# A new attention and convolution list, conditioning products in bursts of eight, a gate broadcast by rounded halves, and shorter one-column sums

## The chip, the core and the metric

The kernel runs on one core of a Trainium2 chip. A core has a matrix engine (TensorE, PE in the profile, with its weight loads as PEld), a vector engine (VectorE, DVE), an activation engine (ScalarE, ACT), a general engine (GpSimd, POOL) and a queue engine that issues most transfers (SyncE, SP). Each works through its own list of instructions in order and waits at semaphores for the others. The metric is the time of one execution on the device in microseconds; lower is better.

## What is computed

One layer of a hybrid backbone on 512 latent and 128 context tokens, all in float32 (D = 1024):

```python
mod = (silu(cond) @ w_ada + b_ada)            # cond: c for latents, c_ctx for context
sh1, sc1, g1, sh2, sc2, g2 = split(mod, 6)
h = rms(x, norm_mix) * (1 + sc1) + sh1
q, k, v, gb, gc, u = split(h @ w_in)          # 8 q heads, 2 kv heads of 64; 3 x 512 for the convolution
q, k = rms(q), rms(k)                         # per head; rotary on latents
attn = softmax(q k^T / 8) v                   # latents read cached context keys and all latents, context reads itself
y_conv = gb * conv3(gc * u)
x = x + g1 * (concat(rms(attn), rms(y_conv)) @ w_out)
h2 = rms(x, norm_ffn) * (1 + sc2) + sh2
x = x + g2 * ((silu(h2 @ w_gate) * (h2 @ w_up)) @ w_down)
```

Outputs are the new x of both token sets and the context's k and v.

## The kernel before

Tokens stand in five tiles of 128 (`t` 0 to 3 latents, 4 = `CTX`). Float32 products are done in three passes: each operand is split into a rounded part (`fp32r`, `hi`) and the rest (`lo`), and `mm3` issues hi·hi, hi·lo and lo·hi. `split` puts the rounding on ScalarE and the subtraction on VectorE. A product of two plain float32 operands is built as two records instead.

Four stages follow each other. First (0 to about 56 us) the conditioning for the first norm, the transposition of x, and q. Then the attention and convolution stage (to about 259 us), which the change is in. Then the output projection in two halves of 512 columns, `j` = 0 and 1. Last the feed-forward part, from about 323 us to the end.

In the second stage the order of TensorE is written by hand, as a list `SEQ` of tokens. `k`, `K`: keys and values of a tile, and the transposition of its keys. `q`, `Q`: norm and rotary of a tile's queries on the other engines, and their transposition. `a`, `t`, `o`: context attention's scores, transposition, products. `Su.h`, `Tu.g`, `Ou.g`: scores of head h, transposition and value product of key group g of latent unit u (16 units: tile, kv head, pair of heads). `r`: the one-column sums of a tile's output norm. `F1`: one filler step. The fillers (84 steps) come from a generator: 12 convolution blocks (`conv_mm`, L675 to L677) of six steps, and after each of them one step of `ada_all`, which computes the conditioning of the sections 2, 3 and 4 (the first gate, the second shift and scale; two halves of 512 columns each).

`ada_all`: a section half takes eight products of 32 rows and 512 columns (`cond_mm`, L377), which go to four column strips of the array in turn. They stand as four in one filler step and four in the next. The result `res` is copied by ScalarE. For the gate it is spread over all partitions by a product with `selT` (L737), once for latents and once for context; for the others four small products with `sel` follow (L742). This second part stands at the head of the next step, ahead of the next section's first four products.

`att_rms` (L900) sums the squares `osq` of a tile's attention output over its four blocks of 128 with four products against a column of ones. `conv_rms` does it for the convolution and gives `rB`, which the first mixing step of the projection needs.

The orders of the other engines come from a scheduler that goes by priorities: `early(n)` raises the priority of what is issued under it. `SOON` stands at the softmax steps and at the splits of transposed probabilities, `SOW` at the splits of weights (negative: later). Weight tiles come in rings: `WFB` = 3 loaded ones, `WHB` = 4 split ones, and `AWB` loaded tiles of conditioning weights; each holds two of a section's eight blocks. PSUM in this stage: two buffers of tag `t` for transpositions and sums, three of `c`, one of `o`, one double one of `s` for scores.

Of the kernel before, what the change touches and what calls it, by code (L numbers as in the profile page):

```python
# [10 lines left out]
F32R = mybir.dt.float32r  # L11
AF = mybir.ActivationFunctionType
ALU = mybir.AluOpType
AX = mybir.AxisListType

P = 128
# [18 lines left out]
P1PRE = ('r0 r1 r2 x0 r3 x1 v0 x2 a0 w0 x3 m0 r4 h00 a1 q02 q01 x4 q00 m1 h01 h10 a2 q03 h11 p0 q04 c0')  # L35
XB = 3
XTE = [0, 1, 0, 1, 1, 1, 0, 1, 1, 0]
SEQ = ('k1 c0 q4 k4 C0 k0 K4 Q4 q0 a0 F1 k2 a1 K0 t0 k3 t1 o0 K1 F1 Q0 o1 K2 F1 K3 F1 S0.0 F1 F1 S0.1 '
# [10 lines left out]
GCUT = [0, 6, 12, 17, 22]  # L49
GB = 6  # L50
SOP = [20, 0]
# [9 lines left out]
RSP = 0  # L61
# [8 lines left out]
PHB = 2  # L70
XP = 50
XPL = 400
TAT = (0, 1)
AWB = 2
AO = 6
SOON = 150
SOW = -300
NA = [0, 1]
QTB = 3
WFB = 3  # L80
# [8 lines left out]
def build(ctx, tc, x_prompt, x_sample, c, cache_k, cache_v, c_ctx, norm_mix, norm_ffn, w_ada, b_ada,  # L89
# [3 lines left out]
    act, dve, pool, pe, sp = nc.scalar, nc.vector, nc.gpsimd, nc.tensor, nc.sync  # L93
# [4 lines left out]
    def open_pool(name, side, names):  # L98
        g = tc.tile_pool(name=name, bufs=1, side=side, reuse_waits="tile")
        pools[name] = (g, g.__enter__())  # L100
        for n in names.split():
            where[n] = name
# [14 lines left out]
    def T(tag, shape, dt=F32, bufs=1):  # L117
        seq[0] += 1
        return pools[where.get(tag, "A")][1].tile(list(shape), dt, tag=tag, bufs=bufs, name=f"{tag}_{seq[0]}")
# [21 lines left out]
    def f32(ap):  # L141
        return ap.bitcast(F32)

    def early(n):
        return tc.high_priority(n)

    def split(hi, lo, src):
        act.activation(hi, src, AF.Copy)  # L148
        dve.tensor_tensor(lo, src, f32(hi), ALU.subtract)  # L149
# [65 lines left out]
    def load(e, later=False):  # L215
# [4 lines left out]
        a, b = src.shape[1], src.shape[2]  # L220
        wf = T("aw", (P, a, b), F32, AWB) if ring == "a" else T("wf", (P, a, b), F32, WFB)
        sp.dma_start(wf, src)
# [73 lines left out]
    for gi, grp in enumerate(GROUPS):  # L296
        for f in grp:
            ph = 2 if f < NPLAIN else 3
# [59 lines left out]
    ones = T("ones", (P, P))  # L358
# [11 lines left out]
    dve.tensor_copy(cp[:, :, 0:2], cs)  # L370
    sel = T("sel", (P, CG))
    dve.tensor_reduce(sel, ident.rearrange("p (g c) -> p c g", c=CG), AX.X, ALU.add)
    selT = T("selT", (P, 2, P))

    def cond_mm(out, k, w):
        g = k % 4
# [17 lines left out]
    def mod_evict(i, f0, n, ps_sc, ps_sh):  # L394

        no = (V_MIX, V_FFN)[i]
        bo = (0, 24)[i]
        if ps_sc is not None:
            tmp = T("modt", (P, n, 2), F32, 2)
            dve.tensor_tensor(tmp, ps_sc, vec[:, no + f0:no + f0 + n].unsqueeze(2).to_broadcast([P, n, 2]), ALU.mult)  # L400
            dve.tensor_tensor(modA[i][:, f0:f0 + n, :], tmp,
                              nb[:, i, f0:f0 + n].unsqueeze(2).to_broadcast([P, n, 2]), ALU.add)
        if ps_sh is not None:
            dve.tensor_tensor(modB[i][:, f0:f0 + n, :], ps_sh,
                              vec[:, bo + f0:bo + f0 + n].unsqueeze(2).to_broadcast([P, n, 2]), ALU.add)
# [142 lines left out]
        else:  # L548
            act.activation(qraw[t], qacc[t], AF.Copy)
    close_pool("B0")  # L550
    open_pool("B2", "left", "vt KA KB VS qT pr ph pl osq c25 aw es")
    phase[0] = 1
    close_pool("psum")
    open_psum("pp2", {"t": PT, "c": 5 - PT, "o": 1, "s": 1})
# [7 lines left out]
    for nm, g in (("q", q_norm), ("k", k_norm)):  # L562
# [5 lines left out]
        r4 = rs_.rearrange("p t (a b c) -> p t a b c", a=2, b=2)  # L568
# [36 lines left out]
    KA = T("KA", (P, NKV, 768), F32R)  # L605
    KB = T("KB", (P, NKV, 768), F32R)
    VS = T("VS", (P, 6, NKV, 2, HD), F32R)
# [109 lines left out]
        yield from ada_some(1)  # L717

    def ada_all():
        for sec, j in ADA:  # L720
            rp = PB(tag="c")
            for h in range(4):
                w = W(("ada", sec, j, h))
                for i in range(2):
                    cond_mm(rp, 2 * h + i, w[:, i])
                if h == 1:
                    yield
            res = T("rs5", (P, 512))
            with early(RSP) if RSP else ExitStack():
                act.activation(res, rp, AF.Copy)  # L730
            if sec == 2:
                sp.dma_start(res[2:3], b_ada[0:1, sec * D + j * 512:sec * D + (j + 1) * 512])
            yield
            if sec == 2:
                for cc in range(2):
                    ps = PB(tag="c")
                    pe.matmul(ps, selT[:, cc], res, start=True, stop=True)  # L737
                    act.activation(g1[cc][:, j * 512:(j + 1) * 512], ps, AF.Copy)
            else:
                ps = PB((P, 4, 2), tag="c")  # L740
                for f in range(4):
                    pe.matmul(ps[:, f], res[:, f * P:(f + 1) * P], sel[:, 0:2], start=True, stop=True)  # L742
                if sec == 4:
                    mod_evict(1, 4 * j, 4, ps, None)
                else:
                    mod_evict(1, 4 * j, 4, None, ps)

    ada_gen = ada_all()

# [28 lines left out]
    qT = [None] * NT  # L778
    oe, osq = {}, {}
    mix_ctx = [T("m0", (P, 4, P), F32R, 2) for _ in range(2)]  # L780

    def att_s(u, h):
# [7 lines left out]
        nm = T("nm", (P, 1), F32, 4)  # L790
        with early(SOON):
            dve.tensor_reduce(nm, s_in, AX.XY, ALU.max, negate=True)
        pr = T("pr", (P, NKEY), F32, PRB)
        sm = T("sm", (P, 1), F32, 4)
        with early(SOON):
            act.activation(pr.rearrange("p (a b) -> p a b", a=2), s_in, AF.Exp, bias=nm, accum_out=sm)
        rsm = T("rsm", (P, 1), F32, 4)
        with early(SOON):
            dve.reciprocal(rsm, sm)
# [8 lines left out]
    def att_t(u, g):  # L808
# [7 lines left out]
        pl = T("pl", (P, 2, 2, P), F32R, PHB)[:, :n]  # L816
        with early(SOON):
            split(ph, pl, tp)
# [24 lines left out]
    def att_add(t, v, e):  # L843

        esw = T("es", (P, 2, P))
        sp.dma_start(esw[0:64], e[64:128, :, 0, :])
        sp.dma_start(esw[64:128], e[0:64, :, 1, :])
        if v == 0:
            of[t] = T("of", (P, 4, P), F32, NT)
            osq[t] = T("osq", (P, 4, P), F32, OSQ) if t != NL - 1 else T("oz", (P, 4, P))  # L850
        o = of[t][:, 2 * v:2 * v + 2]
        dve.tensor_tensor(o[0:64], e[0:64, :, 0, :], esw[0:64], ALU.add)
        dve.tensor_tensor(o[64:128], e[64:128, :, 1, :], esw[64:128], ALU.add)
        act.activation(osq[t][:, 2 * v:2 * v + 2], o, AF.Square)
        if t == CTX:
            split(mix_ctx[0][:, 2 * v:2 * v + 2], mix_ctx[1][:, 2 * v:2 * v + 2], o)

# [20 lines left out]
    def ctx_t(v):  # L878
# [4 lines left out]
        pl = T("pl", (P, GRP, P), F32R, PHB)  # L883
        with early(SOON):
            split(ph, pl, tp)
# [10 lines left out]

    def att_rms(t):
        sps = PB((P, 1))
        for p in range(4):
            pe.matmul(sps, osq[t][:, p], ones[:, 0:1], start=(p == 0), stop=(p == 3))  # L900
        rA[t] = rstd_of(sps, 1, 1.0 / 512, tag="rA")

    def unit(t, v, p):
# [10 lines left out]
    def rms_of(t):  # L914
        if t == CTX or t >= 0:
# [5 lines left out]
             "a": ctx_s, "t": ctx_t, "o": ctx_o, "r": att_rms}  # L921
    for x in SEQ.split():
        if "." in x:
# [30 lines left out]
    def h2_turn(t):  # L954
        cc = 1 if t == CTX else 0
        for g in range(2):
# [4 lines left out]
            for i in range(4):  # L961
                k = 4 * g + i
                with early(XPL):
                    act.activation(h2[g][:, i, FPOS[t]:FPOS[t] + P], tp[:, i], AF.Identity,
# [64 lines left out]
    for j in range(2):  # L1029
        cols = slice(j * 512, (j + 1) * 512)  # L1030
        for n, t in enumerate(TORD[j]):
            cc = 1 if t == CTX else 0
            c0 = t * P + (2 if t == CTX else 0)
            ms = [mix_ctx if t == CTX else mix_half(of[t]), mix_half(yf[:, :, c0:c0 + P])]
            ab = PS2()
            for half in range(2):
                for p in range(4):
                    wh, wl = W(("o", j, 2 * half + p // 2))
                    mm3(ab[:, half], ms[half][0][:, p], ms[half][1][:, p], wh[:, p % 2], wl[:, p % 2],
                        p == 0, p == 3)  # L1040
                    if j == 1 and n >= 2 and (half, p) == TAT:
                        h2_turn(TORD[1][n - 2])
                        if n == 3:
                            b_lo(0, 256)
                        if n == 4:
                            with early(XPL):
                                b_lo(256, HALF)
# [9 lines left out]
            if j == 0:  # L1057
                x2[t] = T("x2", (P, D), F32, NT)
                sp.dma_start(x2[t], x_dram[t])
            with early(XP if j == 0 else XPL):  # L1060
                m = T("mix", (P, 512), F32, 2)
# [5 lines left out]
            if j == 1:  # L1067
                with early(XPL):
                    x2n[t] = T("x2n", (P, D), F32, 2)
# [218 lines left out]
```

## Time and profile before

| | |
|---|---|
| median of 3 runs | 760.46 us (760.42 to 761.08) |
| the profiled execution | 759.46 us |
| its span in the profile | 757.7 us |
| instructions in the profile | 13163 |

The times of rows are those of the profiled execution, from the start of its span. Rows of a timeline give start, length, engine, line, operation, and in brackets the idle time just before with what ended it. The end of a matmul is modelled, so that lengths of matmuls overlap and prices are better read from start to start. A chain of waits gives start, length and what was on it. A table of stretches gives busy time with the number of instructions.

### The profile page before, as it was taken

To read this page: it belongs to the slowest core of one execution; us is meant where nothing else is said; L and a number is where in the kernel's file an instruction comes from. 1 tells how busy PE (TensorE), PEld (TensorE's weight loads), DVE (VectorE), ACT (ScalarE), POOL (GpSimd) and SP (SyncE) were. 2 spreads that over 40 slices of the span, in tenths; PEclk is the share of its full clock that TensorE was granted. 3 is DMA by queue.
4 is the path that set the end of the run, shared out by engine and by line. 5 is a ranking of instruction groups with operands and counts; after the bars stand their busy time and mean duration, and the time that the engine had idled before them with its cause. 6 is when DMAs were issued, how large, how long until landed. Compare 5 with 4: busy or idle time off the path is not lost.

```text
span 757.7 us, 13163 instructions
## 1 busy us (share of the span) xinstructions
PE 734.8 (97%) x5225; PEld 688.8 (91%) x5225; DVE 556.9 (73%) x993; ACT 377.0 (50%) x716; POOL 49.6 (7%) x77
## 2 busy tenths in 40 slices
PE   4998999999999999999999999999999999999997
PEld 3677888989998887889999999999999999999997
DVE  5566987676665799779879778874577866788663
ACT  5455767566656435896552225653125542255510
POOL 2104201011000150000000000000000000000000
PEclk9999999999999999999999999999999999999999
DMA  9994133522433464031235313133213232222312
GB/s 288 310 248 133 43 112 92 171 93 91 142 124 91 133 222 139 1 112 56 84 89 176 112 56 111 57 112 112 57 56 90 79 112 68 73 84 85 112 56 84
DMA packets 102354, 84.60 MB, mean 112 GB/s; under 512 B 4526, under 2 KB 82674, under 8 KB 102292
## 3 DMA queue, kind: packets, MB, share of 16 engines
q1 hardware_dynamic: 100980, 83.39, 36.4%
q8 instruction: 41, 0.67, 0.4%
q10 hardware_dynamic: 1056, 0.26, 0.2%
q0 software_dynamic: 256, 0.11, 0.1%
q14 instruction: 21, 0.17, 0.1%
HBM read 79.68 MB, written 2.75 MB: 109 GB/s over the span
## 4 chain that ended last, share of the span: by engine, by line
PE 83%; DVE 7%; DMA 4%; SPq 2%; ACT 1%; issue 1%; POOL 1%; ACTq 0%; DVEq 0%; POOLq 0%
PE pf L1189 19%; PE pf L153 12%; PE pf L154 12%; PE pf L152 12%; PE pc L675 3%; PE pc L677 3%; PE pc L676 3%; PE po L831 3%; PE ps L788 2%; PE ps L152 2%; PE pt L814 2%; PE ps L154 2%; PE ps L153 2%; PE pc L377 2%; DMA af<-in_w_ada_dram 2%
## 5 line engine op out<-in xcount | busy, mean ns | idle before, releaser
L1189 PE MATMUL pf<-wh,gT 128*128 128x256 f32 x880 | 137.1, 277 | 0.0
L1189 PEld LDWEIGHTS pf<-wh,gT 128*128 128x128 f32 x880 | 117.1, 188 | 0.5 <-issue 0.2
L148 ACT ACTIVATE wh<-wf 128x1024 fp32r<-128x1024 f32 (+1 forms) x76 | 64.3, 846 | 90.0 <-PE pf L1189 45.1
L1189 PE MATMUL pf<-wl,gT 128*128 128x256 f32 x440 | 86.5, 276 | 0.0
L149 DVE TENSOR_TENSOR wl<-wf,wh 128x1024 fp32r<-128x1024 f32 (+1 forms) x42 | 49.2, 1172 | 27.6 <-ACT wh L148 23.4
L1189 PEld LDWEIGHTS pf<-wl,gT 128*128 128x128 f32 x440 | 66.6, 188 | 0.0
L675 PE MATMUL pc<-hH,wh 128*128 128x384 f32 (+1 forms) x192 | 61.5, 320 | 0.2 <-DVE modt L400 0.2
L676 PE MATMUL pc<-hL,wh 128*128 128x384 f32 (+1 forms) x192 | 59.5, 310 | 0.0
L677 PE MATMUL pc<-hH,wl 128*128 128x384 f32 (+1 forms) x192 | 59.4, 309 | 0.0
L152 PE MATMUL pf<-T,wl 128*128 128x320 f32 x160 | 49.2, 308 | 0.0
L153 PE MATMUL pf<-T,wl 128*128 128x320 f32 x160 | 49.2, 308 | 0.0
L154 PE MATMUL pf<-T,wl 128*128 128x320 f32 x160 | 49.2, 308 | 0.0
L152 PE MATMUL pf<-T,wh 128*128 128x320 f32 x160 | 49.2, 308 | 0.0
L153 PE MATMUL pf<-T,wh 128*128 128x320 f32 x160 | 49.2, 308 | 0.0
L154 PE MATMUL pf<-T,wh 128*128 128x320 f32 x160 | 49.2, 308 | 0.0
L152 PE MATMUL pf<-B,wl 128*128 128x320 f32 x152 | 47.0, 309 | 0.0
L153 PE MATMUL pf<-B,wl 128*128 128x320 f32 x152 | 46.8, 308 | 0.0
L154 PE MATMUL pf<-B,wl 128*128 128x320 f32 x152 | 46.8, 308 | 0.0
L148 ACT ACTIVATE wl<-wf 128x512 fp32r<-128x512 f32 x34 | 21.6, 635 | 43.4 <-PE pf L1189 35.5
L152 PE MATMUL pf<-B,wh 128*128 128x320 f32 x136 | 41.9, 308 | 0.0
L153 PE MATMUL pf<-B,wh 128*128 128x320 f32 x136 | 41.9, 308 | 0.0
L154 PE MATMUL pf<-B,wh 128*128 128x320 f32 x136 | 41.9, 308 | 0.0
(278 smaller groups left out, 1958.6 us busy)
## 6 DMA issues: line engine op xcount, KB each, us to landing
wf<-in_w_gate_up_dram SPq DMA_DIRECT2D x44, 512.0 KB, 3.9
aw<-in_w_ada_dram SPq DMA_DIRECT2D x24, 512.0 KB, 4.8
wf<-in_w_down_dram SPq DMA_DIRECT2D x20, 512.0 KB, 3.6
wf<-in_w_in_dram SPq DMA_DIRECT2D x18, 512.0 KB, 6.0
af<-in_w_ada_dram SPq DMA_DIRECT2D x32, 256.0 KB, 6.0
x<-in_x_sample_dram SPq DMA_DIRECT2D x8, 512.0 KB, 4.9
wf<-in_w_out_dram SPq DMA_DIRECT2D x8, 512.0 KB, 4.3
wf<-in_w_ada_dram SPq DMA_DIRECT2D x8, 512.0 KB, 3.7
```

The source lines that it names most:

```text
L148: act.activation(hi, src, AF.Copy)
L149: dve.tensor_tensor(lo, src, f32(hi), ALU.subtract)
L152: pe.matmul(out, lh, rh, start=start, stop=False, skip_group_check=more)
L153: pe.matmul(out, lh, rl, start=False, stop=False, skip_group_check=more)
L154: pe.matmul(out, ll, rh, start=False, stop=stop, skip_group_check=more)
L377: pe.matmul(out[CG * g:CG * (g + 1)], cp[:, k], w, start=(k < 4), stop=(k >= KD - 4), skip_group_check=True)
L675: pe.matmul(acc, wh[:, k], hH[k][:, c0:c0 + n], start=(k == 0), stop=False)
L676: pe.matmul(acc, wh[:, k], hL[k][:, c0:c0 + n], start=False, stop=False)
L677: pe.matmul(acc, wl[:, k], hH[k][:, c0:c0 + n], start=False, stop=(k == KD - 1))
L788: pe.matmul(s2[:, g, :320], q, kk[:, v, P + g * 320:P + (g + 1) * 320], start=(i == 0), stop=(i == 1))
L831: pe.matmul(ov, w, x[:, i].rearrange("p a q -> p (a q)"), start=(g == 0 and i == 0 and n == 0), stop=(last and i == len(kts) - 1 and n == 1))
L1189: pe.matmul(ps[:, c:c + 256], l, r[:, i, c0 + c:c0 + c + 256], start=f == grp[0] and a == 0 and c == 0, stop=f == grp[-1] and a == 2, skip ...
```

## The change

Besides the list `SEQ`, which is written anew from `a0` on, four things. `ada_all` yields once at its head, then does all eight products in one step and the second part in the next one; `AWB` goes from 2 to 4. The gate's `res` is split into `rh` and `rl`, `selT` is rounded (it holds zeros and ones), and each spread is two products of rounded operands. After the second kv head of a tile GpSimd adds the two halves of `osq`, so that `att_rms` needs two products. The priorities of softmax steps and of weight splits move apart.

```diff
-SEQ = ('k1 c0 q4 k4 C0 k0 K4 Q4 q0 a0 F1 k2 a1 K0 t0 k3 t1 o0 K1 F1 Q0 o1 K2 F1 K3 F1 S0.0 F1 F1 S0.1 '
-       'q1 F1 F1 S1.0 F1 T0.0 S1.1 T0.1 T0.2 O0.0 F1 O0.1 O0.2 S2.0 T1.0 F1 T1.1 T1.2 S2.1 O1.0 F1 F1 '
...
+SEQ = ('k1 c0 q4 k4 C0 k0 K4 Q4 q0 a0 k2 F1 a1 t0 K0 k3 K1 o0 t1 F1 Q0 K2 o1 K3 F1 S0.0 F1 F1 S0.1 F1 q1 '
+       'F1 F1 S1.0 F1 T0.0 S1.1 T0.1 F1 T0.2 O0.0 O0.1 S2.0 O0.2 T1.0 F1 T1.1 O1.0 S2.1 T1.2 F1 Q1 F1 '
...
+GSE = 0
-AWB = 2
+AWB = 4
-SOON = 150
-SOW = -300
+SOON = 640
+SOW = -850
...
-    selT = T("selT", (P, 2, P))
+    selT = T("selT", (P, 2, P), F32R)
...
     def ada_all():
+        yield
         for sec, j in ADA:
             rp = PB(tag="c")
             for h in range(4):
                 w = W(("ada", sec, j, h))
                 for i in range(2):
                     cond_mm(rp, 2 * h + i, w[:, i])
-                if h == 1:
-                    yield
             res = T("rs5", (P, 512))
-            with early(RSP) if RSP else ExitStack():
-                act.activation(res, rp, AF.Copy)
+            act.activation(res, rp, AF.Copy)
...
             if sec == 2:
+                hi, lo = T("rh", (P, 512), F32R), T("rl", (P, 512), F32R)
+                with early(GSE):
+                    split(hi, lo, res)
                 for cc in range(2):
                     ps = PB(tag="c")
-                    pe.matmul(ps, selT[:, cc], res, start=True, stop=True)
+                    pe.matmul(ps, selT[:, cc], hi, start=True, stop=False)
+                    pe.matmul(ps, selT[:, cc], lo, start=False, stop=True)
                     act.activation(g1[cc][:, j * 512:(j + 1) * 512], ps, AF.Copy)
...
+            yield
...
         act.activation(osq[t][:, 2 * v:2 * v + 2], o, AF.Square)
+        if v:
+            pool.tensor_tensor(osq[t][:, 0:2], osq[t][:, 0:2], osq[t][:, 2:4], ALU.add)
...
-        for p in range(4):
-            pe.matmul(sps, osq[t][:, p], ones[:, 0:1], start=(p == 0), stop=(p == 3))
+        for p in range(2):
+            pe.matmul(sps, osq[t][:, p], ones[:, 0:1], start=(p == 0), stop=(p == 1))
```

TensorE at the first gate spread, before: `rs` is the section's result, `aw` conditioning weights of the next section, `pt` transposed probabilities `pr`.

```order
L814 MATMUL pt_1636<-ident_76,pr_1544 128x128
L737 MATMUL pc_1647<-rs_351_1467,selT_142 128x512
L737 MATMUL pc_1650<-rs_351_1467,selT_142 128x512
L377 MATMUL pc_1653<-aw_1459,cp_84 32x512 x2
L377 MATMUL pc_1653<-aw_1463,cp_84 32x512 x2
L814 MATMUL pt_1662<-ident_76,pr_1437 128x128
```

And TensorE after the change, first at the first burst of a section with the context tile's sums behind it:

```order
L792 MATMUL ps_1439<-KB_695,qT_1119 128x320 x2
L378 MATMUL pc_1455<-aw_704,cp_84 32x512 x2
L378 MATMUL pc_1455<-aw_718,cp_84 32x512 x2
L378 MATMUL pc_1455<-aw_1243,cp_84 32x512 x2
L378 MATMUL pc_1455<-aw_1245,cp_84 32x512 x2
L906 MATMUL pt_1471<-ones_130,osq_1095 128x1 x2
```

Then at the first gate spread:

```order
L818 MATMUL pt_1635<-ident_76,pr_1550 128x128
L739 MATMUL pc_1650<-rh_1646,selT_142 128x512
L740 MATMUL pc_1650<-rl_1647,selT_142 128x512
L739 MATMUL pc_1654<-rh_1646,selT_142 128x512
L740 MATMUL pc_1654<-rl_1647,selT_142 128x512
L818 MATMUL pt_1658<-ident_76,pr_1446 128x128
```

The burst that stood right behind the gate spread now stands a filler block later, as one of eight products; the sums are two instead of four.

VectorE at the first latent unit, before: `of` is the context attention's output, `KB` the keys' low part from a transposition, `wl` a split of convolution weights, `nm` the maximum of the first scores.

```order
L853 TENSOR_TENSOR of_1096<-t_260_1091,es_1093 64x256
L622 CAST KB_695<-pt_1145 128x2x128
L164 TENSOR_SCALAR rs_1224<-rs_1224 128x8
L598 TENSOR_TENSOR pl_1229<-of_665,tab_682 128x16x16
L149 TENSOR_TENSOR wl_1473<-wf_1470,wh_1472 128x1024
L149 TENSOR_TENSOR m_171_702<-of_1096,m_170_701 128x256
L622 CAST KB_695<-pt_1159 128x2x128
L852 TENSOR_TENSOR of_1096<-t_269_1135,es_1137 64x256
L853 TENSOR_TENSOR of_1096<-t_269_1135,es_1137 64x256
L792 TENSOR_REDUCE nm_1181<-ps_1176 128x1
```

VectorE at the same place after the change:

```order
L857 TENSOR_TENSOR of_1094<-t_258_1089,es_1091 64x256
L623 CAST KB_695<-pt_1132 128x2x128
L623 CAST KB_695<-pt_1153 128x2x128
L165 TENSOR_SCALAR rs_1225<-rs_1225 128x8
L150 TENSOR_TENSOR m_171_702<-of_1094,m_170_701 128x256
L599 TENSOR_TENSOR pl_1230<-of_665,tab_682 128x16x16
L796 TENSOR_REDUCE nm_1172<-ps_1167 128x1
L150 TENSOR_TENSOR wl_1485<-wf_1482,wh_1484 128x1024
```

The two KB follow each other, and the weight split stands behind the maximum.

GpSimd at the end of the stage after the change (`oz` is the last tile's squares, `rB` the convolution's norm):

```order
L717 TENSOR_TENSOR ysum_700<-ysum_700,c_776_3243 128x512
L717 TENSOR_TENSOR ysum_700<-ysum_700,c_776_3243 128x128
L860 TENSOR_TENSOR oz_3033<-oz_3033 128x256
L163 TENSOR_TENSOR rB_3347<-ms_3345,neghalf_132 128x5
L1071 TENSOR_TENSOR mix_3383<-mix_3383,g_167_698 128x512
```

Before, `rB` stood right behind the two `ysum` rows; the add of `oz` is new ahead of it.

More of the change, by code (lines that the diff above doesn't have):

```diff
@@ L550, in build @@
     close_pool("B0")
-    open_pool("B2", "left", "vt KA KB VS qT pr ph pl osq c25 aw es")
+    open_pool("B2", "left", "vt KA KB VS qT pr ph pl osq c25 aw es rh rl")
     phase[0] = 1
```

18 rows, old and new, of the table SEQ are left out of this document.

## Prediction

> **What bounds the kernel now.** I read the page's first part and its chain, then the busy times by stage, then who keeps TensorE waiting, then rows of the timeline for the prices.
>
> ```profile
> span 757.7 us, 13163 instructions
> PE 734.8 (97%) x5225; PEld 688.8 (91%) x5225; DVE 556.9 (73%) x993; ACT 377.0 (50%) x716; POOL 49.6 (7%) x77
> PE 83%; DVE 7%; DMA 4%; SPq 2%; ACT 1%; issue 1%; POOL 1%; ACTq 0%; DVEq 0%; POOLq 0%
> ```
>
> TensorE (PE) holds 83% of the chain that ended last: most time taken from its stream is time taken from the kernel. The stretches of 56 to 75, 75 to 106, 106 to 268 and 268 to 300 us say where this holds (busy us and instruction counts of PE, PEld, DVE, ACT, POOL; then granted clock, DMA share, GB/s):
>
> ```profile
> 56.00:75.00 19.00, 16.90 (x117) 14.97 (x116) 12.31 (x38) 10.53 (x27) 8.76 (x14) 1.00 0.45 135
> 75.00:106.00 31.00, 28.24 (x203) 25.21 (x203) 28.31 (x70) 22.19 (x59) 5.22 (x8) 1.00 0.32 94
> 106.00:268.00 162.00, 161.29 (x1153) 145.45 (x1152) 111.24 (x222) 98.82 (x201) 15.15 (x25) 1.00 0.37 114
> 268.00:300.00 32.00, 31.78 (x137) 24.67 (x136) 30.76 (x43) 14.18 (x23) 8.88 (x6) 1.00 0.58 194
> ```
>
> The attention and convolution list runs from 56 to some 259 us. From 106 us on TensorE is full and VectorE (DVE) has a third of its time free. In 75 to 106 VectorE is the fuller one (28.31 of 31), and there TensorE waits. From 268 to 300, in the output projection, both are full. After that the diff touches nothing. What TensorE itself waited for in the stage (us in total, times, longest), and one wait of ScalarE (ACT):
>
> ```profile
> PE ps L788 <- DVE KB L622: 1.2, 1, 1.2
> PE pt L814 <- DVE pl L149: 0.7, 1, 0.7
> PE pt L655 <- ACT qT L656: 0.7, 1, 0.7
> PE po L831 <- DVE pl L149: 0.4, 1, 0.4
> PE ps L788 <- ACT pr L796: 0.4, 1, 0.4
> ...
> ACT wh L148 <- PE pc L676: 3.1, 3, 1.5
> ```
>
> So two things can move the time: the work in TensorE's stream, and these few waits.
>
> **Bursts of eight.** Before, each of six conditioning sections runs its eight products (L377, four at a time in the four column strips of the array) in two bursts of four, in two filler steps. Now all eight stand in one step, the first ada step of the list is empty and the last burst stands in the last step. The work is the same, so only the edges can be saved:
>
> ```profile
> 25.21 1.07 PE L377 MATMUL pc<-af,cp 128*32 128x256 f32 x16
> 26.21 0.50 PE L152 MATMUL ps<-wh,hH 128*128 128x512 f32 x1
> ...
> 97.48 0.45 PE L788 MATMUL ps<-KB,qT 128*128 128x320 f32 x2
> 97.86 1.06 PE L377 MATMUL pc<-aw,cp 128*32 128x512 f32 x8
> 98.86 0.44 PE L675 MATMUL pc<-hH,wh 128*128 128x384 f32 x1
> 99.14 0.34 PE L676 MATMUL pc<-hL,wh 128*128 128x384 f32 x1
> 99.32 0.34 PE L677 MATMUL pc<-hH,wl 128*128 128x384 f32 x1
> ...
> 100.86 0.45 PE L788 MATMUL ps<-KB,qT 128*128 128x320 f32 x2
> 101.15 0.34 PE L675 MATMUL pc<-hH,wh 128*128 128x384 f32 x1
> ```
>
> Ends of matmuls are modelled, so I go from start to start. Two score products took 0.38 us ahead of a burst (97.48 to 97.86) and 0.29 elsewhere (100.86 to 101.15): 0.09 to get in. The first convolution product behind it took 0.28 (98.86 to 99.14), the next 0.18: 0.10 to get out. Within, a burst of four took 1.00; eight products of half the width took 1.00 as well (25.21 to 26.21), so there the fixed part is nothing; the gate's records below stream 512 columns in 0.43, which makes two rounds 0.86 and the fixed part 0.14. I take 0.10, nearer to the larger since its width is the same. A section saves 0.29, six save 1.7 (ends 0.19 and 0.33: 1.1 to 2.0). The Trainium skill, page "TensorE: Matmul & The Clock Gate", section "Part 3: Packing small matmuls — row/col tiling", has a pack cost one matmul's duration plus some 4 ns for each further tile. By that rule two packs cost the same together or apart and this term would be 0, with the time at 756.2; the rows show the 0.19 at the edges, so they decide. The loads of a section (four of 512 KB) now need four buffers, which they get. They pass convolution weights on the in-order queue of SP, but ScalarE's splits of those wait for TensorE to free their buffers (3.1 us above): they are early, and a load that is some us later costs nothing.
>
> **Gate broadcast by halves.** Two sections each end in two full-precision products against selT, two records each. Now each is two products of rounded halves, one record each, as the 512-column products of the projection are; these start 0.24 apart (second fence, from the chain of waits):
>
> ```profile
> 118.25 0.95 PE L900 MATMUL pt<-ones,osq 128*128 128x1 f32 x8
> 119.05 0.63 PE L814 MATMUL pt<-ident,pr 128*128 128x128 f32 x4
> ...
> 128.51 1.88 PE L737 MATMUL pc<-rs,selT 128*128 128x512 f32 x4
> 130.33 1.06 PE L377 MATMUL pc<-aw,cp 128*32 128x512 f32 x8
> ```
>
> ```profile
> 318.86 0.23 PE ps L152
> 319.10 0.24 PE ps L153
> ```
>
> 1.82 us (128.51 to 130.33) less 0.09 for the entry of the burst behind is 1.73; four records at 0.24 make 0.95; saved 0.78, twice 1.6 (1.4 to 1.7). The split adds one ScalarE and one VectorE instruction of 512 columns per section. A whole filler block lies between burst and gate, and VectorE has 50 us free in 106 to 268, which covers it.
>
> **Fewer one-column sums.** Each of five normalizers took eight records in 0.80 us (118.25 to 119.05); four records take 0.40. Five times is 2.0; the last one stands in the stretch where VectorE is full as well and may be worth nothing (1.6 to 2.2, by 0.11 a record). The price is an add on GpSimd (POOL) per normalizer, below.
>
> **The new order of the list.** Up to a0 (about 75 us) it is the same, and the waits there stay. Then, at the first latent unit (DVE and PE rows, the latter with the idle time in brackets):
>
> ```profile
> 91.74 0.42 DVE L622 CAST KB<-pt 128x256 fp32r<-128x256 f32 x1
> 92.25 0.42 DVE L598 TENSOR_TENSOR pl<-of,tab 128x256 f32<-128x256 f32 x1
> 92.59 1.22 DVE L149 TENSOR_TENSOR wl<-wf,wh 128x1024 fp32r<-128x1024 f32 x1
> 94.06 0.42 DVE L622 CAST KB<-pt 128x256 fp32r<-128x256 f32 x1
> 94.53 0.41 PE L788 MATMUL ps<-KB,qT 128*128 128x320 f32 x1 [1.19 <-DVE KB L622]
> 105.13 0.44 PE L814 MATMUL pt<-ident,pr 128*128 128x128 f32 x2 [0.70 <-DVE pl L149]
> 74.16 0.53 PE L655 MATMUL pt<-identr,qT 128*128 128x128 f32 x4 [0.69 <-ACT qT L656]
> ```
>
> The last KB stood behind a rotary product and a weight split on VectorE. With weight splits at lower priority the two KB now follow each other and the split stands behind nm: the KB comes some 1.9 us sooner and the 1.19 goes. T0.2 needed the buffer of T0.0 after 1.0 us of other work and waited 0.70; a filler step of six 384-column products (0.18 each, 99.14 to 99.32 above) now stands between: it goes. Against that, K2 now follows Q0 at once, with one transposition group between it and the buffer's former use, as at 74.16: up to 0.7 comes. Net -1.2. Covers of the later units (score to score, transposition to product) have a shortest of 2.0 and 1.5 us by the same counting, before 1.8 and 1.2, so I expect no worse there; but 84 fillers have moved and I keep 0.5 for a wait I can't see: -0.7. Ends: -2.7 (the four waits of DVE and of pr all go), +2.7 (as many new ones).
>
> **The sum.** -1.7 - 1.6 - 2.0 - 0.7 = -6.0 on the profiled execution's 759.46, which has 1.76 outside its span: 753.5. The median of the runs stands 1.0 above that execution: 760.46 - 6.0 = 754.5.
>
> **Rivals.**
> (a) The work goes and the new order's waits give part of it back: 5.3 of work less 1.5 to 3.8 of waits, 756.7 to 759.0. For it: the list is new from 75 us on and TensorE has no slack. Against it: VectorE is 69% and ScalarE 61% busy in 106 to 268, and the covers got longer.
> (b) The adds on GpSimd hold up VectorE.
>
> ```profile
> L566 POOL TENSOR_TENSOR tab<-pr,gnq 128x256 f32<-128x256 f32 x1 | 0.7, 728 | 37.1 <-DMA pr<-rope_c_dram 37.1
> L149 DVE TENSOR_TENSOR mL<-of,mH 128x512 fp32r<-128x512 f32 x8 | 7.7, 956 | 0.7 <-ACT mH L148 0.7
> L149 DVE TENSOR_TENSOR mL<-y,mH 128x512 fp32r<-128x512 f32 x10 | 6.8, 682 | 0.2 <-ACT mH L148 0.2
> ```
>
> The same split takes 956 ns on average where GpSimd's gate products run beside some of them, and 682 elsewhere. An add of this size took 0.73, so five hold VectorE at most 3.6 us, and only two fall where it is nearly full: the context tile's and the last tile's, which in addition stands ahead of rB in GpSimd's queue, and rB lets the projection's first mix go. That costs 0.7 to 1.5: 755.2 to 756.0. The Trainium skill, page "SBUF — State Buffer", section "SBUF: two separate sides", says that GpSimd and a VectorE operation with two SBUF inputs exclude each other for a whole instruction; the two rows agree with it.
> (c) Slower: the softmax chains become the bound. Each of the sixteen latent units goes score, maximum, exponential, scaling, transposition, split, product over three engines with two transposition buffers and one score buffer. If the denser stream exposes 0.5 us in each, 8 us come: 762.5. It decides from 0.47 us a unit, since 7.5 have to come back and more. Against it: those units show 0.4 us of named waits after 106 us.
> (d) The saved work isn't on the path, since the projection behind it is held by VectorE (30.76 of 32) with its own backlog. VectorE sat idle waiting for TensorE until the last units, so it moves with it; if not, 759 to 762.
>
> **How the numbers follow.** Sum as worked out (752 to 756.5, with (b) inside): 0.64. (a) 0.20. (d) and a full give-back, within 0.2% (1.5 us, about what a measurement of this kernel can tell from no change): 0.09. (c) 0.07. Faster by more than that is the first two, 0.84; within it 0.09; slower 0.07. The range reaches from the most work with the largest gain in waits (5.9 + 2.7: 751.9, taken as 751.7) to the end of (a), 759.0; it leaves out some 0.17.
>
> **What would show it.** Right: L377 in six bursts of sixteen records of some 1.9 us; the gate's four records 0.24 apart; four records per sum; no wait of L788 for KB; the stage's end some 6 us earlier and the rest of the trace shifted as a whole. Wrong: new waits of L814, L831 or L788 on pl, pr or qT of more than 3 us in total; GpSimd's rB late and a gap on VectorE behind it; a projection that is longer by what the stage lost.

## The result, and the profile after

The changed kernel took 753.12 us (median of 4 runs, 751.29 to 755.38) against 760.77 of the kernel before (4 runs): ratio 0.989, interval 0.986 to 0.993. Measured a second time it took 752.28 (6 runs, 750.99 to 757.0) against 763.75 (23 runs): 0.987, 0.983 to 0.990. The forecast was 754.5 in a range of 751.7 to 759.0: the direction and the range held, and the time was overestimated by 1.4 to 2.2 us. As a difference, 6.0 us was forecast and 7.7 and 11.5 were measured; in the second measurement the kernel before itself ranged from 759.0 to 767.4.

The page of the profile of after, whose execution took 752.2 us: span, engines, chain by engine.

```profile
span 750.4 us, 13147 instructions
PE 729.3 (97%) x5205; PEld 688.0 (92%) x5205; DVE 556.4 (74%) x995; ACT 378.6 (50%) x718; POOL 52.7 (7%) x82
PE 87%; DMA 4%; ACT 3%; DVE 2%; SPq 1%; POOL 1%; issue 1%; ACTq 0%; POOLq 0%; DVEq 0%
```

TensorE has 20 instructions fewer (five sums, eight records to four) and 5.5 us less busy time; VectorE's part of the chain fell from 7% to 2%. The table of stretches, columns as before:

```profile
75.00:106.00 31.00, 29.95 (x205) 28.24 (x205) 28.15 (x71) 23.09 (x60) 6.18 (x9) 0.94 0.21 61
106.00:262.00 156.00, 155.87 (x1139) 143.34 (x1140) 112.63 (x226) 99.70 (x203) 17.70 (x29) 1.00 0.38 124
```

In 75 to 106 TensorE is busy for 29.95 of 31 where it was 28.24; part of that is slower work, since the granted clock there is 0.94 (more on it at the end). What TensorE waited for from 56 us to the stage's end:

```profile
PE pt L620 <- ACT osq L612: 1.2, 2, 0.9
PE pt L656 <- ACT qT L657: 0.7, 1, 0.7
PE pt L656 <- DVE pl L150: 0.4, 1, 0.4
PE pt L620 <- ACT qT L657: 0.3, 1, 0.3
PE pt L620 <- DVE osq L613: 0.2, 1, 0.2
PE ps L792 <- ACT pr L800: 0.2, 1, 0.2
```

The rows for osq and the first one for qT lie ahead of `a0`, as before. The wait for KB (1.2) and those of L814 and L831 for pl (0.7, 0.4) are gone, and so are two small ones of before that the prediction did not list: 0.4 at L881, in the context attention's transposition, for wh, and 0.2 at L675 for modt. New is a wait at Q0 and K2 (L656 for pl, L620 for qT). The edited work itself, TensorE's timeline:

```profile
113.43 0.45 PE L792 MATMUL ps<-KB,qT 128*128 128x320 f32 x2
113.82 1.92 PE L378 MATMUL pc<-aw,cp 128*32 128x512 f32 x16
115.67 0.61 PE L906 MATMUL pt<-ones,osq 128*128 128x1 f32 x4
116.14 0.37 PE L835 MATMUL po<-ph,VS 128*128 128x256 f32 x1
...
127.84 0.48 PE L739 MATMUL pc<-rh,selT 128*128 128x512 f32 x1
128.16 0.40 PE L740 MATMUL pc<-rl,selT 128*128 128x512 f32 x1
128.39 0.39 PE L739 MATMUL pc<-rh,selT 128*128 128x512 f32 x1
128.62 0.39 PE L740 MATMUL pc<-rl,selT 128*128 128x512 f32 x1
128.85 0.60 PE L818 MATMUL pt<-ident,pr 128*128 128x128 f32 x4
```

A burst of eight takes 1.85 us from its start to the next instruction's (113.82 to 115.67), a gate spread 1.01 (127.84 to 128.85, records 0.23 apart behind the first), a sum 0.47.

### The profile page after: what moved, and what is told of

It reads as the page before. It is cut to its first block, busy times and chain, and to the rows that moved or that the text cites. A ratio compares the mean times of both kernels' runs of the same rounds, so it can differ in the third digit from the quotient of the medians.

```text
span 750.4 us, 13147 instructions
## 1 busy us (share of the span) xinstructions
PE 729.3 (97%) x5205; PEld 688.0 (92%) x5205; DVE 556.4 (74%) x995; ACT 378.6 (50%) x718; POOL 52.7 (7%) x82
## 4 chain that ended last, share of the span: by engine, by line
PE 87%; DMA 4%; ACT 3%; DVE 2%; SPq 1%; POOL 1%; issue 1%; ACTq 0%; POOLq 0%; DVEq 0%
PE pf L1195 20%; PE pf L154 12%; PE pf L155 12%; PE pf L153 12%; PE pc L676 4%; PE pc L677 4%; PE pc L678 4%; DMA af<-in_w_ada_dram 3%; PE ps L153 3%; PE po L835 3%; PE ps L792 3%; PE ps L154 3%; PE ps L155 3%; PE pt L818 2%; PE pc L378 2%
## 5 line engine op out<-in xcount | busy, mean ns | idle before, releaser
L1195 PE MATMUL pf<-wh,gT 128*128 128x256 f32 x880 | 137.1, 277 | 0.0
L1195 PEld LDWEIGHTS pf<-wh,gT 128*128 128x128 f32 x880 | 117.1, 188 | 0.5 <-ACT wh L149 0.2
L1195 PE MATMUL pf<-wl,gT 128*128 128x256 f32 x440 | 86.5, 276 | 0.0
L1195 PEld LDWEIGHTS pf<-wl,gT 128*128 128x128 f32 x440 | 66.6, 188 | 0.0
L150 DVE TENSOR_TENSOR pl<-pt,ph 128x512 fp32r<-128x512 f32 (+1 forms) x50 | 30.0, 602 | 19.7 <-ACT ph L149 19.5
L153 PE MATMUL pf<-B,wh 128*128 128x320 f32 x136 | 41.9, 308 | 0.0
L154 PE MATMUL pf<-B,wh 128*128 128x320 f32 x136 | 41.9, 308 | 0.0
```

The lines of the kernel that those rows point to most:

```text
L153: pe.matmul(out, lh, rh, start=start, stop=False, skip_group_check=more)
L154: pe.matmul(out, lh, rl, start=False, stop=False, skip_group_check=more)
L1195: pe.matmul(ps[:, c:c + 256], l, r[:, i, c0 + c:c0 + c + 256], start=f == grp[0] and a == 0 and c == 0, stop=f == grp[-1] and a == 2, skip ...
```

## The experiments

Single executions of one kernel scatter by several us (the last section shows two things that differ between profiles). The kernel before took 760.0 to 763.8 us on the chips used, and each ratio is to its runs on the same chip. Beside the medians I use a length inside the traces: from the first product of `a0` to the first product of the projection. A window of half clock inside it is taken off with 1.5 us: a0 to a1 took 6.95 us in the profile of after, which has such a window there, and 5.45 in its repeat, which has none. In us:

```
kernel                             a0 at  mix at  length  windows  less 1.5 each   median
before                             74.53  258.72  184.19     0         184.2       760.0 to 763.8
after                              74.92  252.59  177.67     1         176.2       753.1
after, repeated                    74.11  250.78  176.67     0         176.7       752.3
work only (old list)               74.96  260.58  185.62     1         184.1       761.3
work, new priorities (old list)    75.09  263.83  188.74     3         184.2       760.9
list and priorities only           75.17  258.13  182.96     0         183.0       760.6
after, old priorities              75.67  252.08  176.41     0         176.4       754.2
work, old list, 4 fillers moved    77.09  258.40  181.31     0         181.3       760.7
after, covers taken away           75.14  253.92  178.78     0         178.8       756.0
after, bursts of four              74.02  256.28  182.26     1         180.8       756.6
after, full-precision gate         74.18  253.29  179.11     0         179.1       754.4
after, four-product sums           74.06  252.21  178.15     0         178.2       753.6
after, no adds                     74.88  251.36  176.48     0         176.5       753.4
after, two fillers in the head     77.01  263.47  186.46     2         183.5       764.2
```

**The work alone, and the order alone.** The first has every edit of the work and the old order:

```diff
-SEQ = (the new list)
+SEQ = (the list of before)
-SOON = 640
-SOW = -850
+SOON = 150
+SOW = -300
```

> The changed kernel with the list SEQ and the two priorities (SOON, SOW) of before: the bursts of eight, the halved gate products and the two-product sums alone. Theory (the gain is work taken from TensorE's stream): 5.3 us less than before, 755.0 to 756.0, and the waits of L788 for KB and of T0.2 come back as before. Rival (the gain is the new order's): 759 to 761.

The second is the kernel before with the new list and the new priorities, nothing else.

> The kernel before with the list and the two priorities of after, no other edit (the empty first step is not there, so each conditioning burst stands where the list has its filler). Theory: the order alone is worth the waits that go, 0.7 to 2 us: 758.7 to 760. Rival (the order is the larger part): 755 to 757. Rival (the new order fits only the shorter work): 761 or more.

Work alone: 761.29 us, ratio 1.002 (1.000 to 1.004). Order alone: 760.58, ratio 1.000 (0.998 to 1.002). Neither gains anything that can be measured, while both together gain 7.7. The expectation for the work alone missed by 5 us. That for the order alone (758.7 to 760) was missed as well, just short of its rival that the new order fits only the shorter work (761 or more). Where the saved work went is seen in the trace of the work alone, first TensorE at the two gate spreads, then VectorE at the first. The last fence has TensorE at the first gate spread in the kernel before:

```profile
129.85 0.48 PE L739 MATMUL pc<-rh,selT 128*128 128x512 f32 x1
...
130.63 0.39 PE L740 MATMUL pc<-rl,selT 128*128 128x512 f32 x1
130.86 0.60 PE L818 MATMUL pt<-ident,pr 128*128 128x128 f32 x4
131.96 0.38 PE L835 MATMUL po<-ph,VS 128*128 128x256 f32 x1 [0.50 <-ACT ph L149]
133.94 0.38 PE L835 MATMUL po<-pl,VS 128*128 128x256 f32 x1 [1.60 <-DVE pl L150]
...
163.05 0.40 PE L740 MATMUL pc<-rl,selT 128*128 128x512 f32 x1
165.38 0.44 PE L818 MATMUL pt<-ident,pr 128*128 128x128 f32 x2 [1.93 <-DVE pl L150]
```

```profile
131.60 1.22 DVE L150 TENSOR_TENSOR wl<-wf,wh 128x1024 fp32r<-128x1024 f32 x1
132.74 0.55 DVE L807 TENSOR_SCALAR pr<-pr,rsm 128x640 f32<-128x640 f32 x1
133.20 1.28 DVE L150 TENSOR_TENSOR pl<-pt,ph 128x512 fp32r<-128x512 f32 x2
```

```profile
131.32 0.66 PE L814 MATMUL pt<-ident,pr 128*128 128x128 f32 x4
...
132.52 0.39 PE L831 MATMUL po<-pl,VS 128*128 128x256 f32 x1 [0.42 <-DVE pl L149]
```

In the old list the gate spread stands between T3.0 and T3.1, with O3.0 right behind. Before, spread and burst took 2.8 us there together (128.51 to 131.32), and in that time ScalarE and VectorE split the probabilities for O3.0; now the spread takes 1.0 (129.85 to 130.86) and the burst is elsewhere. TensorE comes to O3.0 early and waits 0.5 us for ph and 1.6 for pl, which stands behind a weight split and a scaling on VectorE. The first product with pl starts as long after the start of the spread as before, 4.1 us against 4.0, though 1.8 us of work between them are gone: VectorE sets its time. At T6.2 the wait is 1.93. At the first product of the projection 0.6 more is waited, for the copy of the last burst's result. What was taken out of TensorE's work had also been the time in which the softmax of the next product was done. The new list has a filler and S4.1 between T3.1 and O3.0, and T6.1 behind the spread, with a filler ahead of O6.0.

**Which half of the order: priorities or list.** The changed kernel again as a base, then with the old priorities alone, then the work and the old list with the new priorities.

> The changed kernel as it is, for a base on the chip of the next three. Theory (work and list only pay together, since the list gives the shortened gate spreads new covers): 752 to 755 us as before, some 7 below the kernel before. Rival (its 753.1 was luck of one chip, the pieces do nothing): 758 to 761.

> The changed kernel with the old priorities alone (SOON 150, SOW -300). The trace of the work alone under the old list shows VectorE splitting weights (1.22 us) ahead of a probability's split at both gate spreads. Theory (the list's covers matter, the priorities little): 753 to 755, with the 1.2 us wait for KB back. Rival (the priorities are what pays: weight splits stand in the softmax's way again): 757 to 760.

> All the work, old list, new priorities. Theory (list's covers): still 758 to 761, as the two waits at the gate spreads (1.9 and 2.1 us) stay within 1 us of what they were. Rival (priorities): these waits go and it comes to 754 to 756.

The changed kernel with the old priorities: 754.21 us, ratio 0.988 (0.984 to 0.991), length 176.4 as in the repeat (176.7). The old list with the new priorities: 760.87, ratio 0.998 (0.995 to 1.001), and the same waits to a tenth, from its table of waits:

```profile
PE pt L818 <- DVE pl L150: 2.3, 2, 1.9
PE po L835 <- DVE pl L150: 1.6, 1, 1.6
PE ps L792 <- DVE KB L623: 1.2, 1, 1.2
```

The priorities do nothing that these runs can tell; the list does it. The wait for KB, too, stays with the old list and is absent with the new one, whichever the priorities, though I had expected the old ones to bring it back. VectorE around the last KB, with the old list and new priorities, then with the new list and old priorities:

```profile
93.85 0.42 DVE L623 CAST KB<-pt 128x256 fp32r<-128x256 f32 x1
...
94.70 1.22 DVE L150 TENSOR_TENSOR wl<-wf,wh 128x1024 fp32r<-128x1024 f32 x1
...
96.17 0.42 DVE L623 CAST KB<-pt 128x256 fp32r<-128x256 f32 x1
```

```profile
92.75 0.76 DVE L623 CAST KB<-pt 128x256 fp32r<-128x256 f32 x2
```

With the old list the weight split stands between the two KB at low priority as well; with the new list the two follow each other at high priority as well.

**Covers given back to the old list.** All the work, old list, old priorities, four fillers moved by a few places:

```diff
-T3.0 F1 T3.1 O3.0 F1 T3.2 S4.1 F1 F1 O3.1
+T3.0 F1 T3.1 F1 F1 O3.0 T3.2 S4.1 F1 O3.1
-T6.0 T6.1 F1 T6.2 O6.0 S7.1 F1 F1 F1 O6.1
+T6.0 T6.1 F1 F1 F1 T6.2 O6.0 S7.1 F1 O6.1
```

> All the work, old list and old priorities, and only four filler steps moved by a few places: two now stand between T3.1 and O3.0 behind the first gate spread, and two more between the second gate spread and T6.2. In the trace of the work alone TensorE waits there 1.9 and 2.1 us for VectorE's split, where the longer gate spread and the burst behind it had stood before. Theory (a filler step is also a cover, and the shortened one uncovers the softmax chain): both waits fall under 0.5 us and the time falls by 3 to 4 us, to some 757 to 758. Rival (VectorE is the bound there, whatever TensorE does): the waits come up at the next unit and the time stays at 760 to 761.

TensorE there, from T3.1 over the first of the fillers' products to their last, O3.0, and S5.0:

```profile
131.37 0.60 PE L818 MATMUL pt<-ident,pr 128*128 128x128 f32 x4
131.72 0.42 PE L676 MATMUL pc<-hH,wh 128*128 128x384 f32 x1
...
134.80 0.34 PE L678 MATMUL pc<-hH,wl 128*128 128x384 f32 x1
134.98 0.28 PE L835 MATMUL po<-ph,VS 128*128 128x256 f32 x1
135.10 0.28 PE L835 MATMUL po<-pl,VS 128*128 128x256 f32 x1
...
138.83 0.56 PE L792 MATMUL ps<-KA,qT 128*128 128x320 f32 x2 [0.89 <-ACT pr L800]
```

Both waits are gone; one of 0.89 has come up at S5.0. The length fell from 184.1 to 181.3: 2.8 of the 4.0 us that stood in the two waits, for a move of four fillers. The median doesn't show it: 760.68 (755.4 to 762.51), ratio 0.996 (0.993 to 0.999), against the 757 to 758 expected. The profiled run has the slow pace of the last section, which is worth 4.2 us in it; how many of the others had it their times don't tell. So the mechanism is shown in the trace, and the gain in the time stays unproved.

**Covers taken from the new list.** The reverse, on the changed kernel:

```diff
-T3.0 F1 T3.1 F1 S4.1 O3.0 F1 T3.2
+T3.0 F1 T3.1 O3.0 F1 T3.2 S4.1 F1
-T6.0 F1 T6.1 F1 O6.0 T6.2
+T6.0 T6.1 F1 T6.2 O6.0 F1
```

> The changed kernel, with only the tokens around the two gate spreads put as the old list has them: O3.0 ahead of the filler and of S4.1, and T6.0 T6.1 ahead of the spread with T6.2 right behind it. Theory (the shortened spread uncovers the softmax chain unless fillers stand there): the waits of 1.9 and 2.1 us come back at these two places, and the time rises by 3 to 4 us, to 755.5 to 757. Rival (the new list is better everywhere, no single place matters): under 1 us.

755.97 us, ratio 0.993 (0.991 to 0.996), as expected; but the length went up only from 176.7 to 178.8, by 2.1 of the 3 to 4 us. From its waits behind 106 us, where the changed kernel has none:

```profile
PE ps L792 <- ACT pr L800: 0.8, 1, 0.8
PE po L835 <- DVE pl L150: 0.8, 1, 0.8
```

The wait at O3.0 is back at half its size, another at S5.0; at T6.2 only 0.2 came. Two places of the list are worth 2.1 us here and 2.8 in the old list, of some 6.4 by which both halves of the change gain more together than apart (184.2 to 176.5, of which the work alone gains 0.1 and the order alone 1.2). The traces name most of this. TensorE's waits between the two landmarks add up to 3.2 us before, 7.1 with the work alone, 2.2 with the order alone and 0.9 with both, which is 5.2 less than the two halves apart would give. Of the 2.2 with the order alone, 1.5 are not there with both: 0.9 at the first gate spread, where the next burst of four waits for ScalarE to empty the gate's buffer, and 0.6 at L675 for modt. The wait for KB is no part of it, since it goes with the order alone as well. The other places were not tried one by one.

**One part of the work undone at a time, new order kept.** Bursts of four with two loaded tiles again:

> The changed kernel with the conditioning products again in two bursts of four and AWB 2. Theory: six entries and exits of a burst come back, 0.27 to 0.29 us each as the trace after shows (inner rounds 0.41 apart, the last one 0.52, 0.09 ahead and 0.1 behind): 1.6 to 1.8 us slower than the changed kernel. Rival (a pack costs the same wherever it stands): no difference.

The gate's `res` in full precision again:

> The changed kernel with the gate spread again by full-precision products against selT. Theory: 0.78 us for each of the two sections, 1.6 us slower than the changed kernel. Rival (the gate's turn is covered by a wait that is there anyway): under 0.5.

The sums over four blocks, without GpSimd's adds:

> The changed kernel with the sums of four products again and without GpSimd's adds. Theory: 20 more records of 0.1 us on TensorE's path, 2.0 us slower than the changed kernel (1.6 to 2.2), 754.3 to 755.3. Rival (the sums were beside other waits): under 0.7 us.

And the adds taken away alone:

> The changed kernel without GpSimd's adds; the sums leave out the second half of the squares, so that TensorE's work is the same. Theory: the adds cost nothing, same within 0.5 us. Rival (they hold up VectorE at the context tile and at the last tile, and delay rB): 0.7 to 1.5 us faster.

Bursts of four: 756.56 us, ratio 0.995 (0.993 to 0.997), length 180.8 against 176.7, so 4.1 us where 1.6 to 1.8 was expected. Full gate: 754.41, 0.992 (0.991 to 0.994), length 179.1: 2.4 where 1.6 was expected. Each has a wait behind 106 us that the changed kernel does not have, first the row of bursts of four, then that of the full gate:

```profile
PE pc L676 <- ACT g L742: 1.7, 2, 1.3
```

```profile
PE ps L788 <- ACT pr L796: 0.6, 1, 0.6
```

Without these waits 2.4 and 1.8 us are left, nearer to what was expected. With bursts of four in the new list, spread and next burst come in one filler step, and the convolution behind them waits until ScalarE has emptied the gate's `c` buffer. So the new list doesn't only serve the new work, it needs it.

Four-product sums: 753.6, 0.992 (0.989 to 0.995). The times can't tell this from the changed kernel, the trace can: from S0.1 to the projection it takes 157.8 us and the repeat of the changed kernel 156.0, in four steps of 0.43 to 0.45 at the four sums of this stretch; in the projection 0.25 more come. That is 2.0. Without the adds: 753.41, 0.991 (0.988 to 0.994), length 176.5 against 176.7, with a chance wait of 0.25 for KB in the repeat; the projection is 0.2 shorter (63.1 against 63.3).

**Fillers for the waits of the head.** At 67 to 75 us TensorE waits in every trace. I tried to put two fillers there:

```diff
-C0 k0 K4 Q4 q0 a0
+C0 k0 F1 K4 F1 Q4 q0 a0
-O14.0 F1 F1 F1 T15.0
+O14.0 F1 F1 T15.0
-T15.1 F1 F1 F1 O14.2
+T15.1 F1 F1 O14.2
```

> The changed kernel with two filler steps taken from the end of the list (from the groups of three around T15) and put ahead of K4 and of Q4, where TensorE waits some 2.9 us in all at 67 to 75 us in every trace. Theory: the two steps (1.06 us each) stand in these waits, and the end of the list has cover to spare: 1.5 to 2.1 us faster than the changed kernel, 750 to 751.5, and fewer half-clock windows right behind them. Rival (fillers there delay the keys on ScalarE and VectorE by as much, or the gate sections that stand two tokens earlier now uncover a unit): 752.5 or more.

764.18 us, ratio 1.004 (1.002 to 1.007): 11 us slower than the changed kernel, and the whole gain gone. The waits of the head are smaller than the 2.9 us of the expectation: 2.1 us in all in the profile of after, 1.5 in its repeat. From the waits of this run between 56 and 265 us:

```profile
PE ps L792 <- ACT pr L800: 4.4, 5, 2.1
PE ps L871 <- ACT pr L879: 1.5, 1, 1.5
```

The fillers come out of one generator, so taking two early makes every later filler token stand for the step two further on. The step that is empty now falls between S0.0 and S0.1, where two full steps had stood, and there TensorE waits 2.1 us; a1 waits 1.5 for ScalarE. In the head itself little is covered: 1.0 us of waits is left there, and `a0` starts at 77.01 us, where the other runs of the new list have it at 74.0 to 75.7, so most of the fillers' time came on top. The list fits the lengths of its fillers one by one, which is the same mechanism once more. No version of these runs beats the changed kernel.

## Why the prediction was right, and where it was not

**Bursts, -1.7: right, a little small.** Two bursts of four took 2.00 from start to start, one of eight takes 1.85: a fixed part of 0.15 where I took 0.10. With the 0.19 of the edges a section saves 0.34, six 2.0. By the rule cited from the Trainium skill this would have been nothing; the rows bear out the edges. That undoing it costs 4.1 is the order's doing: 1.7 of it is the wait for g, and the 2.4 left is near the 2.0.

**Gate, -1.6: right.** 1.73 to 1.01 is 0.72, twice 1.4; the run that undid it lost 2.4, 0.6 of it in a new wait.

**Sums, -2.0: right** in the trace, 2.0 by the run without them.

**Order, -0.7: the direction right, the size and one cause wrong.** From a0 to the feed-forward part the changed kernel is 8.4 us shorter (248.39 to 239.95, the projection's share of that 0.9); less 2.0, 1.4 and 2.0 for the work, some 3.0 are left for the order and the waits, beyond the far end that I gave it (-2.7). I counted two waits as gone, KB and T0.2; the one at L831 went too, and that for pr fell by 0.2, while 0.3 came at K2, where I had feared up to 0.7, and 0.4 at Q0. That is 1.8 net. The small waits that I had not listed (0.4 at L881, 0.2 at L675) and one of 0.2 in the projection went as well, which makes some 2.5, and 0.5 that no row names. The projection's share is hardly the order's: it took 64.2 to 64.6 us in the three profiles with bursts of four (before, order alone, bursts of four again) and 63.1 to 63.5 in all the others. For KB I named the lower priority of weight splits, and the runs with the priorities exchanged show that the list alone does it.

**The sum.** The step that failed is that I added: the work as if TensorE's stream were full in either order, the order as a term by itself. The table says -0.1 and -1.2 us for each alone, -7.5 to -8.0 for both. My sum came near only because I priced the work together with the list that fits it. I did count the covers of the new list; I did not ask what the old one would do with a shorter gate spread, though the prices (2.8 us to 1.0) stood in the rows.

**Rivals.** (a) is out for this list, and its mechanism is just what the work alone does in the old one. (b) is out: the adds cost 0.2 us, not 0.7 to 1.5. (c) is out: no named wait after 106 us. (d) is out: the projection became shorter by 0.9, not longer.

**The signs.** Bursts of sixteen records, records of the gate 0.23 apart, four records a sum, no wait for KB and an end of the stage 6.1 us earlier in the profiled run all came. The rest was shifted as a whole, but for those 0.9 us.

## What to carry to other kernels

In a list written by hand each step is work and cover at once: before a step is shortened, ask which chain on other engines ran under it, and put the cover back in the same edit. Try such an edit and its order in all four combinations, since each half alone can measure as nothing. And where a gain of 2 us lies below the scatter of the times, compare lengths between two landmarks of the traces.

## What the runs showed of the hardware

**Half-clock windows.** In this stage TensorE's granted clock falls to one half for windows of 3.41 us. Rows of the table of stretches: the window of after, the same place in its repeat, and two windows of the old list with new priorities.

```profile
75.50:78.90 3.40, 3.40 (x19) 3.40 (x18) 2.86 (x9) 3.32 (x11) 1.95 (x1) 0.50 0.00 0
```

```profile
74.40:77.80 3.40, 3.40 (x31) 3.40 (x30) 2.81 (x9) 3.37 (x10) 1.94 (x1) 1.00 0.00 0
```

```profile
134.00:137.30 3.30, 3.12 (x11) 3.12 (x12) 2.19 (x5) 0.63 (x1) 0.72 (x5) 0.50 0.57 159
168.00:171.40 3.40, 3.40 (x13) 3.40 (x12) 3.30 (x7) 2.02 (x5) 0.00 (x0) 0.51 0.42 125
```

The window of after has 19 products where the repeat has 31, with TensorE busy throughout in both. The other two belong to the waits of 1.6 and 1.9 us at the gate spreads: one starts 0.3 us before the wait ends, the other 1.0 us behind it, so that a wait can cost its length and 1.5 us more. The work alone has the same waits and no window there.

What differs is where the waits lie. In each trace the windows start whole multiples of 3.413 us apart; with the old list and new priorities they start at 17.85, 75.88, 133.91 and 168.04 us, which is 17, 17 and 10 times that. So time can be cut into steps of this length. The step ahead of the window at 133.91, and the step in which TensorE idles longest at the same place of the work alone:

```profile
130.50:133.91 3.41, 1.58 (x9) 0.97 (x7) 3.41 (x8) 3.31 (x8) 1.83 (x1) 1.00 0.00 0
```

```profile
129.81:133.22 3.41, 2.03 (x12) 1.37 (x10) 3.41 (x8) 3.41 (x10) 1.38 (x1) 1.00 0.00 0
```

TensorE idles 1.8 us in the first and 1.4 in the second, where more of the same waits falls into the next step. At the second gate spread it is 1.9, all in one step and with a window behind it, against 1.4. At 75 us, with 1.0 to 1.1 us idle in the step ahead, some profiles have a window and some have none, so idle time is not all that decides, and no run tested it. The Trainium skill, page "TensorE: Matmul & The Clock Gate", section "HAM oscillation — how this bites in real kernels", asks for no idle gaps above some 3.4 us; here windows followed single waits of 1.6 to 2.1 us.

**Two paces of the down products.** The products of L1195 between 640 and 740 us, in the profile of after and in that of its repeat:

```profile
L1195 PE MATMUL pf<-wh,gT x227: 276/276/281, 639.8 to 740.0; 128*128 128x256 f32 x114
```

```profile
L1195 PE MATMUL pf<-wh,gT x220: 281/281/288, 639.7 to 739.9; 128*128 128x256 f32 x110
```

Same program, same granted clock, no wait, and 220 products against 227 in the same 100 us. From the first down product to the last it is 352.9 us against 348.7. The first 360 of them, up to some 440 us, go alike in both; the others, from some 513 us on, start 0.113 us apart in the one and 0.118 in the other. Five of the fourteen profiles of this study have the slower pace, of five different kernels. I found no cause. Its 4.2 us would make up most of the scatter between executions above, but of an execution without a profile nothing tells the pace.
